# A head's cached keys loaded ahead of the ring into the memory of the attention's output, and a new order of score rows, maxima and query chunks

## The chip, the cores and the metric

The kernel runs on one core of a Trainium2 chip. Its engines are TensorE (PE in the profile; PEld is its weight load), VectorE (DVE), ScalarE (ACT), GpSimd (POOL) and SyncE (SP), which issues most of the loads from HBM. The metric is the device time of one execution in microseconds (us), less is better. The kernel before was run three times: 1280.98, 1282.48 and 1283.21 us, median 1282.48 us.

## The reference

One inference step of two layers for two groups of rows that share all weights: a prompt of 256 rows and 8 sample rows, each with its own cached keys and values. Each layer adds half a SwiGLU block, a mixer (a gated convolution in layer 0, a gated recurrence in layer 1), a cross attention over a memory, and another half SwiGLU block to the row:

```
for i in range(DEPTH):                                   # DEPTH = 2, D_MODEL = 1024, D_FF = 2816
    x = x + 0.5 * swiglu(rmsnorm(x, norm_ffn1[i]), ...)
    x = x + mixer_i(rmsnorm(x, norm_mix[i]))
    x = x + cross_attn(rmsnorm(x, norm_xattn[i]), mem_k[i], mem_v[i], w_xq[i], w_xo[i])
    x = x + 0.5 * swiglu(rmsnorm(x, norm_ffn2[i]), ...)

def cross_attn(x, mk, mv, w_q, w_o):                     # 4 heads of 256, 256 memory rows
    q = (x @ w_q).reshape(B, T, X_HEADS, X_HEAD_DIM)
    s = jnp.einsum('bthd,bnhd->bhtn', q, mk) / math.sqrt(X_HEAD_DIM)
    p = jax.nn.softmax(s, axis=-1)
    return jnp.einsum('bhtn,bnhd->bthd', p, mv).reshape(B, T, D) @ w_o
```

The prompt's memory keys and values are computed in the kernel (`rmsnorm(mem) @ w_kv`, 256 rows). The sample's keys and values are read from the caches, 8 batches x 256 rows x 4 heads x 256 numbers per layer, 8 MB of keys and 8 MB of values.

## The kernel before

All products run in three matmuls of rounded halves, hi x hi, lo x hi and hi x lo (`mm3`, L339 to L341; in the memory's keys and values L987 to L989). Each half chunk of weights is loaded by SP into `raw` (L99, six buffers), rounded by ACT into `wh` (L110), and the rest `wl` is made by DVE or POOL (L125; five buffers each). Prompt and sample rows stand side by side as 264 columns, so that PE has one stream of products from start to end; everything else is fitted between them.

The order is the program's order, as a scheduler with priorities lays it out, with some edges put in by hand (`order(...)`). Side work is written as generators in two lanes of a `Flow`; `flow.tick()` after every few products takes one step of each lane. So a `yield` is a unit of distance: what stands behind it comes one tick later in every engine's order.

The attention of a layer (about 300 to 425 us of the span in layer 0, 960 to 1085 in layer 1) runs so:

- `project` computes the queries, two chunks (two heads) at a time: k steps 0 to 2 of chunk 0, 0 to 2 of chunk 1, then the steps 3 to 7 of both in turn, then the evacuation of both by `evac_q` (L973), which starts the sample's score generator of the head in lane 0.
- `do_kv` computes keys and values of the prompt's memory, head by head, in two banks `kv`. Each head starts three generators in lane 1: `transpose_k` (`pkt` L1017, its copy `KTt` L1021), `prompt_scores` (matmuls `psc` L1070 into a bank, maxima `mxp` L1057 on DVE, two exponentials `Pp` on ACT, L315, reciprocal `zsp` L1060 on DVE, scaling `Pp` L1062 on ACT, transposes `ppt` L1084 on PE, its halves `PTh` and `PTl` L1091), and `prompt_values` (products `po`, outputs `oh` and `ol` L1107).
- `sample_scores(h)`, lane 0: a query transpose `pq` (L1038) and 16 rows on DVE (L1043, one row of keys of all 128 partitions against `pq`, a yield after every fifth), then the maximum `mxs` (L1050) and an exponential.
- `sample_rest`, lane 0, behind the four heads' scores: after SLACK = 5 yields, for each pair of heads 32 multiply-adds on DVE (L1153, L1156) into `acc` and, last, `total`; between them the steps of `combine`, which joins the maxima and sums of the partitions by small matmuls `pst` (L1112, L1119, L1129). Then the matmuls `spt<-oz,total` (L1173), which an edge holds behind the last product put out so far (`flow.passed`), and their evacuation `oh` (L1180, ACT) and `ol` (L1181, DVE).
- `out_proj` multiplies `oh`, `ol` with the output weights; its last two k steps wait for pair 1 of the sample.

The sample's keys and values come through a ring: four tiles of 1 MB, in the order k of heads 0 to 3 (two tiles each), then v of pairs 0 and 1 (four tiles each). `Ring.done` gives a tile back and at once issues the next load (`pump`), on SP, between the weight loads in program order. A load on SP waits until its tile is free and until one of eight outstanding loads has landed, and what stands behind it on SP waits too. The first tiles of a ring are issued while the stage before still runs.

Of the kernel before, what the change touches and what calls it, by code (L numbers as in the profile page):

```python
# [16 lines left out]
P = 128  # L17
# [22 lines left out]
HURRY = 40  # L40
STAGGER = 3
SLACK = 5
# [176 lines left out]
class Ring:  # L219


    def __init__(self, pool):
        self.pool, self.free, self.line, self.tiles, self.n = pool, RING, [], {}, 0

# [12 lines left out]

    def done(self, key):
        del self.tiles[key]
        self.free += 1  # L240
        self.pump()
# [3 lines left out]
def trunk_step(ctx: ExitStack, tc: tile.TileContext, ins, consts, outs, stop=None):  # L245
# [165 lines left out]
    def project(nch, rh, rl, evac, kt_major=2, need=None, before=None, late_lo=False):  # L411
        if not callable(rh):
            rh, rl = (lambda k, t=rh: t[:, k]), (lambda k, t=rl: t[:, k])
        done = 0
        if kt_major:
# [18 lines left out]
            else:  # L434
                order = [(c, k) for c in range(kt_major) for k in range(STAGGER)]
                order += [(c, k) for k in range(STAGGER, KT) for c in range(kt_major)]
                for n, (c, k) in enumerate(order):
                    if before is not None and c == 0:
                        before(k)
                    for j in range(2):  # L440
                        s = slice(j * P, j * P + P)
                        mm3(pss[2 * c + j][2][:, :NC], ws[c](k), rh(k), rl(k), k == 0, k == KT - 1, s)
# [6 lines left out]
            if need is not None:  # L449
                need.ready()  # L450
            with tc.high_priority(offset=HURRY):
                for c, j, ps in pss:
                    evac(c, j, ps[:, :NC])
# [312 lines left out]
    def add_cache(l):  # L766
# [15 lines left out]
        for h in range(XH):  # L782
            for hf in range(2):
                ring.add((l, "k", h, hf), fill_k(h, hf))
# [159 lines left out]
    def attention(l, norm, nxt):  # L944
        with tc.tile_pool(name="at", bufs=1) as ap:
# [83 lines left out]
            def sample_scores(h):  # L1029
# [10 lines left out]
                for i in range(NI):  # L1040
                    t = ring.tiles[l, "k", h, i // 8].rearrange("p (i d) -> p i d", d=XD)
                    junk = ap.tile([P, XD], F32, tag="junk", name="junk", bufs=1)
                    nc.vector.tensor_tensor_reduce(  # L1043
                        junk, t[:, i % 8], pq[:, :XD], 1.0, 0.0, ALU.mult, ALU.add, sc[:, h, i : i + 1]
                    )
# [7 lines left out]
            def softmax(src, npart, rows, name):  # L1053
# [3 lines left out]
                nc.vector.reduce_max(mx, src, axis=AX.X, negate=True)  # L1057
# [37 lines left out]
            def prompt_values(h):  # L1095
# [9 lines left out]
                ohv, olv = oh[:, 2 * h : 2 * h + 2, :T], ol[:, 2 * h : 2 * h + 2, :T]  # L1105
# [34 lines left out]
            def sample_rest():  # L1140
# [4 lines left out]
                for pair in range(XH // 2):  # L1145
# [31 lines left out]
                    with tc.high_priority(offset=HURRY):  # L1177
                        ptv = pt[:, : 4 * NB].rearrange("p (t b) -> p t b", b=NB)
                        ohv, olv = (t[:, 4 * pair : 4 * pair + 4, T:] for t in (oh, ol))
                        nc.scalar.copy(ohv, ptv)  # L1180
                        nc.vector.tensor_sub(olv, ptv, ohv.bitcast(F32))  # L1181
# [10 lines left out]
            project(XH, xh, xl, evac_q, need=norm)  # L1192
            for h in range(XH):
                do_kv(h)
            out_proj(oh, ol, nxt, late=(KT - 2, lambda k: until(k // 4), lambda: flow.drain(1)))
# [490 lines left out]
```

## Time and profile before

| | |
|---|---|
| three runs, us | 1280.98, 1282.48, 1283.21 |
| the profiled execution, us | 1282.15 |
| its span, us | 1280.4 |
| PE busy | 1258.7 us, 98% |
| DVE busy | 842.4 us, 66% |
| ACT busy | 703.4 us, 55% |
| POOL busy | 346.9 us, 27% |
| chain that ended last | PE 91%, DVE 3%, ACT 2%, DMA 2% |
| 1 MB loads of cached keys | 16, median 8.8 us from issue to landing |
| 1 MB loads of cached values | 16, median 9.1 us |

Busy times are of one profiled execution. The span runs from the first instruction to the last; the execution's own time is 1.75 us more. The clock column of a view by windows is the share of TensorE's clock that was granted in that window; over the whole span it was 0.997.

### The profile page before, as it was taken

The page shows a single profiled execution, that of the slowest core. Times are in us where ns is not written, and L with a number is a line of the kernel's source. Part 1 is how long each engine was busy: PE and PEld are TensorE (multiplying, and loading weights), DVE is VectorE, ACT ScalarE, POOL GpSimd, SP SyncE. Part 2 cuts the span into 40 slices and gives each one's busy share as a digit, 9 for nine tenths or more (in the row PEclk, how much of TensorE's full clock was granted, in tenths as well). Part 3 has the DMA queues.
Part 4 walks back from the last instruction along what each step waited for, and adds up shares of the span by engine and source line. Part 5 has one row for each costly group of instructions (what it writes and reads, how often), then busy time and mean ns, then how long its engine had stood idle before and what let it go on. Part 6 is the DMA issues. An engine that isn't in the chain of part 4 may idle for free.

```text
span 1280.4 us, 25535 instructions
## 1 busy us (share of the span) xinstructions
PE 1258.7 (98%) x10039; PEld 1230.7 (96%) x10039; DVE 842.4 (66%) x1625; ACT 703.4 (55%) x1167; POOL 346.9 (27%) x272
## 2 busy tenths in 40 slices
PE   8999999999999999999999999999999999999996
PEld 8999999999789999999999999999999789999996
DVE  7655567758777655546655535887887787766454
ACT  6455544446655645544555544656566666766542
POOL 2211231214864211132111132000016862112220
PEclk9999999999999999999999999999999999999999
DMA  8795556655899666556666556653545997997550
GB/s 274 246 305 177 167 180 190 187 160 178 295 395 318 193 176 189 172 168 191 193 173 191 171 171 190 193 171 122 189 151 172 385 384 248 287 324 227 162 165 35
DMA packets 269898, 270.96 MB, mean 212 GB/s; under 512 B 8777, under 2 KB 259721, under 8 KB 269266
## 3 DMA queue, kind: packets, MB, share of 16 engines
q1 hardware_dynamic: 263870, 263.98, 65.4%
q10 hardware_dynamic: 5908, 5.35, 1.2%
q8 instruction: 79, 1.29, 0.4%
q14 instruction: 41, 0.34, 0.1%
HBM read 259.19 MB, written 10.10 MB: 210 GB/s over the span
## 4 chain that ended last, share of the span: by engine, by line
PE 91%; DVE 3%; ACT 2%; DMA 2%; POOL 1%; issue 1%; SPq 0%; DVEq 0%; POOLq 0%; ACTq 0%
PE pj L340 20%; PE pj L339 20%; PE pj L341 20%; PE dn L339 7%; PE dn L341 7%; PE dn L340 7%; PE kv L987 2%; PE kv L988 2%; PE kv L989 2%; ACT wh L110 1%; DVE wl L125 1%; PE pl L1333 1%; PE psc L1070 1%; DMA ring<-in_cache_mem_k_dram 1%; DVE xl L365 1%; DMA raw<-in_w_xkv_dram 1%
## 5 line engine op out<-in xcount | busy, mean ns | idle before, releaser
L125 DVE TENSOR_TENSOR wl<-raw,wh 128x1024 fp32r<-128x1024 f32 (+1 forms) x334 | 411.7, 1238 | 240.0 <-ACT wh L110 224.2
L339 PE MATMUL pj<-xh,wh 128*128 128x264 f32 x1952 | 557.8, 286 | 0.3 <-DVE g L824 0.3
L340 PE MATMUL pj<-xl,wh 128*128 128x264 f32 x1952 | 553.4, 284 | 0.0
L341 PE MATMUL pj<-xh,wl 128*128 128x264 f32 x1952 | 553.0, 283 | 0.0
L110 ACT CAST wh<-raw 128x1024 fp32r<-128x1024 f32 (+1 forms) x406 | 415.5, 1032 | 215.9 <-PE pj L340 107.8
L339 PEld LDWEIGHTS pj<-xh,wh 128*128 128x128 f32 x1952 | 367.7, 188 | 1.9 <-issue 1.4
L340 PEld LDWEIGHTS pj<-xl,wh 128*128 128x128 f32 x1952 | 368.0, 189 | 0.2
L341 PEld LDWEIGHTS pj<-xh,wl 128*128 128x128 f32 x1952 | 366.1, 188 | 0.0
L125 POOL TENSOR_TENSOR wl<-raw,wh 128x1024 fp32r<-128x1024 f32 (+1 forms) x74 | 173.3, 2356 | 127.2 <-ACT wh L110 108.3
L832 POOL TENSOR_TENSOR al<-a,ah 128x264 fp32r<-128x264 f32 x88 | 90.4, 1029 | 411.2 <-ACT ah L831 411.1
L339 PE MATMUL dn<-ah,wh 128*128 128x264 f32 x704 | 200.9, 285 | 0.0
L341 PE MATMUL dn<-ah,wl 128*128 128x264 f32 x704 | 200.0, 284 | 0.0
L340 PE MATMUL dn<-al,wh 128*128 128x264 f32 x704 | 199.4, 283 | 0.0
L341 PEld LDWEIGHTS dn<-ah,wl 128*128 128x128 f32 x704 | 132.7, 188 | 0.0
L339 PEld LDWEIGHTS dn<-ah,wh 128*128 128x128 f32 x704 | 132.4, 188 | 0.2
L340 PEld LDWEIGHTS dn<-al,wh 128*128 128x128 f32 x704 | 132.5, 188 | 0.0
L315 ACT ACTIVATE g<-g 128x264 f32<-128x264 f32 x88 | 36.9, 424 | 76.6 <-DVE g L824 76.6
L831 ACT CAST ah<-a 128x264 fp32r<-128x264 f32 x88 | 36.0, 413 | 68.2 <-DVE a L830 68.1
L360 ACT ACTIVATE xh<-xT,gains 128x264 fp32r<-128x264 f32 x56 | 28.1, 512 | 72.0 <-DVE xT L858 59.1
L1043 DVE CUSTOM_DVE_ANT_0 junk<-ring,pq 128x256 f32<-128x256 f32 x128 | 53.7, 420 | 12.3 <-DMA ring<-in_cache_mem_k_dram 8.6
L378 POOL TENSOR_TENSOR nacc_norm_xattn<-nacc_norm_xattn,nsq 128x264 f32<-128x264 f32 x14 | 13.6, 972 | 174.8 <-ACT nsq L377 174.5
L1156 DVE SCALAR_TENSOR_TENSOR acc<-ring,sc,acc 128x256 f32<-128x256 f32 x112 | 54.5, 487 | 2.7
(327 smaller groups left out, 1538.7 us busy)
## 6 DMA issues: line engine op xcount, KB each, us to landing
raw<-in_w_ffn_gate_dram SPq DMA_DIRECT2D x88, 512.0 KB, 5.8
raw<-in_w_ffn_up_dram SPq DMA_DIRECT2D x88, 512.0 KB, 4.6
raw<-in_w_ffn_down_dram SPq DMA_DIRECT2D x64, 512.0 KB, 4.1
ring<-in_cache_mem_k_dram SPq DMA_DIRECT2D x16, 1024.0 KB, 8.8
raw<-in_w_xkv_dram SPq DMA_DIRECT2D x64, 256.0 KB, 3.6
ring<-in_cache_mem_v_dram SPq DMA_DIRECT2D x16, 1024.0 KB, 9.1
raw<-in_w_rec_in_dram SPq DMA_DIRECT2D x32, 512.0 KB, 4.3
raw<-in_w_ffn_down_dram SPq DMA_DIRECT2D x32, 384.0 KB, 3.0
```

What stands on the lines that cost most here:

```text
L110: ins = self.behind(self.hi[i % len(self.hi)], copy(wh[:, :n], self.raw[i][:, :n]))
L125: ins = eng.tensor_sub(wl[:, :n], self.raw.pop(i)[:, :n], wh[:, :n].bitcast(F32))
L315: in_line(nc.scalar.activation(dst, src, func, **kw))
L339: nc.tensor.matmul(ps, wh[:, s], rh, start=first, stop=False)
L340: nc.tensor.matmul(ps, wh[:, s], rl, start=False, stop=False)
L341: return nc.tensor.matmul(ps, wl[:, s], rh, start=False, stop=last).ins
L360: W.pin(nc.scalar.activation(xh[:, k, :n], src, AF.Copy, scale=gcol(self.name, self.layer, k)))
L831: nc.scalar.copy(ah[:, blk], a)
L832: nc.gpsimd.tensor_sub(al[:, blk], a, ah[:, blk].bitcast(F32))
L987: nc.tensor.matmul(pss[nt], mh[:, k, t], wh, start=k == 0, stop=False)
L1043: nc.vector.tensor_tensor_reduce(junk, t[:, i % 8], pq[:, :XD], 1.0, 0.0, ALU.mult, ALU.add, sc[:, h, i : i + 1])
L1156: nc.vector.scalar_tensor_tensor(dst, t[:, i % 4, j], p, sums, op0=ALU.mult, op1=ALU.add)
```

## The change

Four things are changed in the attention, the same in both layers. No arithmetic is added or taken away, and the same bytes are loaded.

First, the two key tiles of head 2 (`GUEST`) no longer pass through the ring. When the attention starts, two tiles `spare0` and `spare1` are opened under the same tags as the outputs `oh` and `ol`, with one buffer each, and head 2's keys are loaded into them (`Ring.lodge`). The outputs are opened in the same memory when the first prompt head writes them. The ring then carries the keys of heads 0, 1 and 3, and after them the values, so that each load behind head 1 moves two places forward.

Second, a row of sample scores on DVE comes behind the last `mxp` of the program so far (`ahead`), and the generator yields after every fourth row rather than every fifth. SLACK is 1 in place of 5.

Third, in the query projection, chunk 0 computes its k steps 5 to 7 in one piece and is evacuated before chunk 1 does its own (`split=5`); before, both ended together.

Fourth, the `wl` splits that DVE does later come behind the sample's `ol` (`W.after["v"]`).

```
-SLACK = 5
+GUEST = 2
+SLACK = 1
 class Ring:
+        self.guests, self.lodged = {}, set()
+    def lodge(self, key, t):
+        self.guests.pop(key)(t)
+        self.tiles[key] = t
+        self.lodged.add(key)
     def done(self, key):
         del self.tiles[key]
+        if key in self.lodged:
+            return
         self.free += 1
         self.pump()
...
-    def project(nch, rh, rl, evac, kt_major=2, need=None, before=None, late_lo=False):
+    def project(nch, rh, rl, evac, kt_major=2, need=None, before=None, late_lo=False, split=KT):
+        def out(c):
+            if need is not None:
+                need.ready()
+            with tc.high_priority(offset=HURRY):
+                for j in range(2):
+                    evac(c, j, pss[2 * c + j][2][:, :NC])
...
-                order += [(c, k) for k in range(STAGGER, KT) for c in range(kt_major)]
+                order += [(c, k) for k in range(STAGGER, split) for c in range(kt_major)]
+                order += [(c, k) for c in range(kt_major) for k in range(split, KT)]
...
+                    if split < KT and k == KT - 1:
+                        out(c)
...
-                ring.add((l, "k", h, hf), fill_k(h, hf))
+                if h == GUEST:
+                    ring.guests[l, "k", h, hf] = fill_k(h, hf)
+                else:
+                    ring.add((l, "k", h, hf), fill_k(h, hf))
...
-            oh = ap.tile([P, KT, NC], F32R, name="oh")
-            ol = ap.tile([P, KT, NC], F32R, name="ol")
+            both = {}
+            for hf, tag in enumerate("hl"):
+                t = ap.tile([P, KT, NC], F32, tag="o" + tag, name=f"spare{hf}", bufs=1)
+                ring.lodge((l, "k", GUEST, hf), t.rearrange("p k n -> p (k n)")[:, : 8 * XD])
+            def open_out():
+                for tag in "hl":
+                    both[tag] = ap.tile([P, KT, NC], F32R, tag="o" + tag, name="o" + tag, bufs=1)
...
-            sampled = set()
+            sampled, ahead = set(), []
...
+                    if ahead:
+                        order(row, ahead[-1], "heads ahead of rows")
...
-                    if i % 5 == 4:
+                    if i % 4 == 3:
                         yield
...
-                nc.vector.reduce_max(mx, src, axis=AX.X, negate=True)
+                ahead.append(nc.vector.reduce_max(mx, src, axis=AX.X, negate=True).ins)
...
+                if not both:
+                    open_out()
...
-                        nc.vector.tensor_sub(olv, ptv, ohv.bitcast(F32))
+                        W.after["v"] = nc.vector.tensor_sub(olv, ptv, ohv.bitcast(F32)).ins
...
-            project(XH, xh, xl, evac_q, need=norm)
+            project(XH, xh, xl, evac_q, need=norm, split=5)
```

The kernel's lines move by some 30: the score row is L1043 before and L1075 now, `mxp` L1057 and L1091, `zsp` L1060 and L1094, `psc` L1070 and L1104, `ppt` L1084 and L1118, `spt` L1173 and L1209.

**SP's queue in layer 0's attention, before.** `raw` are halves of weights, `ring9` to `ring12` the key tiles of heads 2 and 3, `ring13` and `ring14` the first two value tiles:

```order
L770 DMA ring9_4084<-in_cache_mem_k_dram 128x8x256
L99 DMA raw116_4144<-in_w_xkv_dram 128x2x256 x2
L770 DMA ring10_4149<-in_cache_mem_k_dram 128x8x256
L99 DMA raw117_4212<-in_w_xkv_dram 128x2x256 x2
L770 DMA ring11_4221<-in_cache_mem_k_dram 128x8x256
L99 DMA raw118_4235<-in_w_xkv_dram 128x2x256 x2
L770 DMA ring12_4258<-in_cache_mem_k_dram 128x8x256
L99 DMA raw119_4272<-in_w_xkv_dram 128x2x256 x2
L99 DMA raw120_4304<-in_w_xkv_dram 128x2x256 x2
L778 DMA ring13_4313<-in_cache_mem_v_dram 128x4x512
L99 DMA raw121_4359<-in_w_xkv_dram 128x2x256 x2
L778 DMA ring14_4364<-in_cache_mem_v_dram 128x4x512
```

The same queue now, at the attention's start and then around head 3's keys and the first values; the row behind the last one shown is `raw120`:

```order
L100 DMA raw108_3776<-in_w_xkv_dram 128x2x256 x2
L792 DMA spare0_3821<-in_cache_mem_k_dram 128x8x256
L792 DMA spare1_3823<-in_cache_mem_k_dram 128x8x256
L100 DMA raw109_3852<-in_w_xkv_dram 128x2x256 x2
L100 DMA raw110_3869<-in_w_xkv_dram 128x2x256 x2
```

```order
L792 DMA ring9_4067<-in_cache_mem_k_dram 128x8x256
L100 DMA raw115_4117<-in_w_xkv_dram 128x2x256 x2
L792 DMA ring10_4128<-in_cache_mem_k_dram 128x8x256
L100 DMA raw116_4150<-in_w_xkv_dram 128x2x256 x2
L100 DMA raw117_4212<-in_w_xkv_dram 128x2x256 x2
L800 DMA ring11_4223<-in_cache_mem_v_dram 128x4x512
L100 DMA raw118_4233<-in_w_xkv_dram 128x2x256 x2
L800 DMA ring12_4260<-in_cache_mem_v_dram 128x4x512
L100 DMA raw119_4270<-in_w_xkv_dram 128x2x256 x2
```

Head 2's two loads stand six weight halves further up, directly behind the first half of the key-value weights; head 3's two take the places in the ring that head 2's had, and the first two value loads those of head 3's. The third value load, before between the key-value weights `raw122` and `raw123`, stands behind the first half of the output weights, `raw124`, now, and the fourth behind the second.

**DVE's queue at head 3's first rows, layer 0.** `sc` are the scores (each row is two instructions there), `mxs` is head 2's maximum, `mxp` the maxima of the prompt's first head. Before:

```order
L1050 TENSOR_REDUCE mxs<-sc 128x1
L1043 ISA junk,sc<-ring_4221,pq 128x256
L1043 ISA sc 128x1
L1043 ISA junk,sc<-ring_4221,pq 128x256
L1043 ISA sc 128x1
L1043 ISA junk,sc<-ring_4221,pq 128x256
L1043 ISA sc 128x1
L1043 ISA junk,sc<-ring_4221,pq 128x256
L1043 ISA sc 128x1
L1057 TENSOR_REDUCE mxp<-psc 128x2
```

Now:

```order
L1084 TENSOR_REDUCE mxs<-sc 128x1
L1091 TENSOR_REDUCE mxp<-psc 128x2
L1075 ISA junk,sc<-ring_4067,pq 128x256
L1075 ISA sc 128x1
L1075 ISA junk,sc<-ring_4067,pq 128x256
L1075 ISA sc 128x1
L1075 ISA junk,sc<-ring_4067,pq 128x256
L1075 ISA sc 128x1
L1094 RECIPROCAL zsp<-zsp 128x2
```

Four rows of head 3 went from ahead of `mxp` to behind it, and the reciprocal stands three rows behind `mxp` as before.

**PE's queue where pair 0 of the sample is handed over, layer 0.** `psc` are head 2's prompt scores, `kv3` head 3's key and value products. Before:

```order
L1070 MATMUL psc_4762<-KTt2_4746,qT2_4022 128x256 x4
L987 MATMUL kv3_0_4723<-wh121_4581,mh_3819 128x512
L988 MATMUL kv3_0_4723<-wl121_4611,mh_3819 128x512
L989 MATMUL kv3_0_4723<-wh121_4581,ml_3820 128x512
L987 MATMUL kv3_1_4724<-wh121_4581,mh_3819 128x512
L988 MATMUL kv3_1_4724<-wl121_4611,mh_3819 128x512
L989 MATMUL kv3_1_4724<-wh121_4581,ml_3820 128x512
L1173 MATMUL spt_4786<-oz_3824,total_4570 128x8 x4
```

Now:

```order
L1021 MATMUL kv3_1_4730<-wh121_4589,ml_3820 128x512
L1209 MATMUL spt_4762<-oz_3826,total_4557 128x8 x2
L1104 MATMUL psc_4769<-KTt2_4746,qT2_4027 128x256
L1209 MATMUL spt_4762<-oz_3826,total_4557 128x8 x2
L1104 MATMUL psc_4769<-KTt2_4746,qT2_4027 128x256 x3
L1019 MATMUL kv3_0_4729<-wh121_4589,mh_3819 128x512
```

The sample's matmuls went from six products behind head 2's scores to the place at which these scores stood, ahead of and among them. Layer 1 has the same rows in the same order at all of these places.

More of the change, by code (lines that the diff above doesn't have):

```diff
@@ L441, in project @@
                         s = slice(j * P, j * P + P)
-                        mm3(pss[2 * c + j][2][:, :NC], ws[c](k), rh(k), rl(k), k == 0, k == KT - 1, s)
+                        flow.passed = mm3(
+                            pss[2 * c + j][2][:, :NC], ws[c](k), rh(k), rl(k), k == 0, k == KT - 1, s
+                        )
+                    if split < KT and k == KT - 1:
+                        out(c)
                     if n % kt_major == kt_major - 1:
@@ L448, in project @@
             W.release()
[L449 to L453, printed above, removed]
+            if split == KT:
+                for c in range(kt_major):
+                    out(c)
             flow.tick()
@@ L1042, in sample_scores @@
                     junk = ap.tile([P, XD], F32, tag="junk", name="junk", bufs=1)
-                    nc.vector.tensor_tensor_reduce(
+                    row = nc.vector.tensor_tensor_reduce(
                         junk, t[:, i % 8], pq[:, :XD], 1.0, 0.0, ALU.mult, ALU.add, sc[:, h, i : i + 1]
                     )
+                    if ahead:
+                        order(row, ahead[-1], "heads ahead of rows")
                     if i % 8 == 7:
                         ring.done((l, "k", h, i // 8))
-                    if i % 5 == 4:
+                    if i % 4 == 3:
                         yield
@@ L1104, in prompt_values @@
                 pov = po.rearrange("p (t n) -> p t n", t=2)
-                ohv, olv = oh[:, 2 * h : 2 * h + 2, :T], ol[:, 2 * h : 2 * h + 2, :T]
+                if not both:
+                    open_out()
+                ohv, olv = (both[tag][:, 2 * h : 2 * h + 2, :T] for tag in "hl")
                 nc.scalar.copy(ohv, pov)
@@ L1178, in sample_rest @@
                         ptv = pt[:, : 4 * NB].rearrange("p (t b) -> p t b", b=NB)
-                        ohv, olv = (t[:, 4 * pair : 4 * pair + 4, T:] for t in (oh, ol))
+                        ohv, olv = (both[tag][:, 4 * pair : 4 * pair + 4, T:] for tag in "hl")
                         nc.scalar.copy(ohv, ptv)
-                        nc.vector.tensor_sub(olv, ptv, ohv.bitcast(F32))
+                        W.after["v"] = nc.vector.tensor_sub(olv, ptv, ohv.bitcast(F32)).ins
                     sampled.add(pair)
@@ L1191, in attention @@
             flow.spawn(1, mem_split())
-            project(XH, xh, xl, evac_q, need=norm)
+            project(XH, xh, xl, evac_q, need=norm, split=5)
             for h in range(XH):
                 do_kv(h)
-            out_proj(oh, ol, nxt, late=(KT - 2, lambda k: until(k // 4), lambda: flow.drain(1)))
+            out_proj(both["h"], both["l"], nxt, late=(KT - 2, lambda k: until(k // 4), lambda: flow.drain(1)))
     GH = 4
```

## The prediction

> **What bounds the kernel now.** I read the page's busy times and its chain of waits first, then PE's waits, and then single instructions around the two longest.
>
> ```profile
> PE 1258.7 (98%) x10039; PEld 1230.7 (96%) x10039; DVE 842.4 (66%) x1625; ACT 703.4 (55%) x1167; POOL 346.9 (27%) x272
> PE 91%; DVE 3%; ACT 2%; DMA 2%; POOL 1%; issue 1%; SPq 0%; DVEq 0%; POOLq 0%; ACTq 0%
> PE ppt L1084 <- ACT Pp L1062: 3.6, 2, 2.3
> PE pj L340 <- DVE ol L1181: 1.4, 2, 0.7
> PE pj L339 <- ACT oh L1180: 0.5, 2, 0.3
> PE psc L1070 <- ACT KTt L1021: 0.3, 1, 0.3
> ```
>
> PE is busy for 98%, and no product is added or removed, so only PE's idle time and its slow time can move the end. The last four rows (PE's waits: total us, times, longest) are what the attentions hold: 3.6 us in which the transposes `ppt` of the first prompt head wait for its scaled probabilities, once in each layer, and 1.9 us at the end of each attention's products for the sample's outputs (1.4 for `ol`, 0.5 for `oh`). The chain that leads to the longer one, layer 0:
>
> ```profile
> 341.52 1.99 PE L1070 MATMUL psc<-KTt,qT 128*128 128x256 f32 x8 [0.35 <-ACT KTt L1021]
> 345.11 0.42 DVE L1043 CUSTOM_DVE_ANT_0 junk<-ring,pq 128x256 f32<-128x256 f32 x1 [2.19 <-DMA ring<-in_cache_mem_k_dram]
> 346.85 0.69 DVE L1057 TENSOR_REDUCE mxp<-psc 128x2 f32<-128x512 f32 x1
> 347.26 0.39 PE L989 MATMUL kv<-wh,ml 128*128 128x512 f32 x1
> 347.57 0.47 ACT L315 ACTIVATE Pp<-psc,mxp 128x256 f32<-128x256 f32 x1 [4.21 <-DVE mxp L1057]
> 348.48 1.04 ACT L110 CAST wh<-raw 128x1024 fp32r<-128x1024 f32 x1
> 349.41 0.91 ACT L1062 ACTIVATE Pp<-Pp,zsp 128x256 f32<-128x256 f32 x2
> 349.98 1.30 PE L1084 MATMUL ppt<-ident,Pp 128*128 128x128 f32 x4 [2.33 <-ACT Pp L1062]
> ```
>
> The scores are there at 341.52 + 1.99 = 343.51, and their maximum starts at 346.85. In between DVE stood at head 3's first row, which waited 2.19 us for its keys, and did four such rows, since they are ahead of `mxp` in its order. From `mxp` everything follows at once, 3.13 us to `ppt`; PE was out of work at 347.26 + 0.39 = 347.65. Layer 1 is the same with shorter waits, 1000.34 + 1.95 = 1002.29 against 1004.56:
>
> ```profile
> 1000.34 1.95 PE L1070 MATMUL psc<-KTt,qT 128*128 128x256 f32 x8
> 1002.82 0.42 DVE L1043 CUSTOM_DVE_ANT_0 junk<-ring,pq 128x256 f32<-128x256 f32 x1 [1.13 <-DMA ring<-in_cache_mem_k_dram]
> 1004.56 0.69 DVE L1057 TENSOR_REDUCE mxp<-psc 128x2 f32<-128x512 f32 x1
> 1007.70 0.94 PE L1084 MATMUL ppt<-ident,Pp 128*128 128x128 f32 x4 [1.30 <-ACT Pp L1062]
> ```
>
> **What the stall costs.** In windows (us, then busy time of PE, PEld, DVE, ACT, POOL with counts, granted clock, DMA share, GB/s):
>
> ```profile
> 347.60:350.00 2.40, 0.07 (x2) 0.02 (x1) 2.26 (x12) 2.40 (x7) 0.40 (x1) 0.98 1.09 388
> 350.00:353.40 3.40, 3.40 (x10) 2.71 (x11) 3.22 (x14) 1.85 (x3) 3.40 (x2) 0.51 1.06 398
> 1007.70:1011.00 3.30, 3.23 (x15) 2.59 (x16) 3.07 (x14) 2.11 (x4) 3.13 (x2) 1.00 1.07 403
> ```
>
> Behind layer 0's gap the clock is granted at 0.51 for 3.40 us, which costs 3.40 x (1 - 0.51) = 1.67 us more; behind the gap of 1.30 us in layer 1 it stays at 1.00. So layer 0's stall is worth 2.33 + 1.67 = 4.00 us and layer 1's 1.30.
>
> That the low clock goes with the gap is read from these two windows alone. The Trainium skill ("TensorE: Matmul & The Clock Gate", Part 1, "What's actually happening") has the clock fall after at least one idle window of about 3.4 us, which runs freely; a gap of 2.33 us would not fill one. By that page the low stretch has another cause and could stay, and the sum would lose its 1.67 us; the trace speaks against it as far as one row can, since the low clock begins where the gap ends.
>
> **Maxima ahead of rows.** The new edge puts `mxp` ahead of head 3's rows. By 345.11 - 2.19 = 342.92 DVE had ended head 2 in layer 0, by 1002.82 - 1.13 = 1001.69 in layer 1, both ahead of the scores' ends, so `mxp` can start at 343.51 and 1002.29, 3.34 and 2.27 us sooner, whatever the loads do. The three rows between `mxp` and `zsp` stay. With the same 3.13 and 3.14 us behind it `ppt` is ready at 346.64 and 1005.43. PE comes to it at 347.65, and in layer 1 at 1007.70 - 1.30 = 1006.40. Both stalls are gone with 1.0 us to spare; a row of 0.42 us or half the weight cast (1.04 us, ahead of `Pp` on ACT) would still fit. Gain: 4.00 + 1.30 = **5.3 us**.
>
> **Head 2's keys ahead of the ring; four rows a step; split queries.** These bring nothing by themselves: they move the sample's chain on DVE forward, and its cover is that DVE then idles at `mxp`. They matter for what follows. The loads:
>
> ```profile
> 306.00:312.00 6.00, 6.00 (x50) 5.86 (x49) 4.46 (x7) 4.21 (x8) 0.62 (x1) 1.00 0.55 172
> 312.00:327.00 15.00, 15.00 (x119) 14.64 (x118) 11.54 (x50) 10.81 (x23) 12.82 (x11) 1.00 0.43 140
> 334.16 0.57 SPq L770 DMA_DIRECT2D ring<-in_cache_mem_k_dram  x1
> 346.25 0.37 SPq L778 DMA_DIRECT2D ring<-in_cache_mem_v_dram  x1
> 351.77 0.40 SPq L778 DMA_DIRECT2D ring<-in_cache_mem_v_dram  x1
> 359.02 1.07 SPq L99 DMA_DIRECT2D raw<-in_w_xo_dram  x1
> L125 POOL TENSOR_TENSOR wl<-raw,wh 128x1024 fp32r<-128x1024 f32 (+1 forms) x74 | 173.3, 2356 | 127.2 <-ACT wh L110 108.3
> ```
>
> The two spare loads (2 MB) go where the DMA share is 0.55 and 0.43, so the weights behind them on SP are not made late; in exchange head 3's second load (334.16) and the first value load (346.25) start when the slots two places ahead come free, by head 1's rows rather than head 2's, 16 rows of 0.42 us or 6.7 us sooner at least. The spare tiles wait for the last readers of the outputs' memory, the stage before, so SP isn't held. Where this leaves a loss is the third value load (351.77): it now stands behind the first output weight half on SP, which was issued at 359.02. It needs the buffer that POOL's split behind the cast of 348.48 frees, and before it also stood behind a fourth value load that waited for its ring slot. With `mxp` 3.34 us sooner the cast is at 345.14 to 346.18, and with one or two splits of 2.36 us (last row, the page's group) the buffer is free by 348.5 to 350.9; the fourth value load is now behind it. I put the third value load at about 351, where it is now.
>
> **The sample's handover, one step of order sooner.** SLACK 1 puts `spt` where `psc` of head 2 begins:
>
> ```profile
> 376.59 1.89 PE L1070 MATMUL psc<-KTt,qT 128*128 128x256 f32 x8
> 379.70 0.95 PE L1173 MATMUL spt<-oz,total 128*128 128x8 f32 x8
> 376.84 0.87 DVE L1156 SCALAR_TENSOR_TENSOR total<-ring,sc,acc 128x256 f32<-128x256 f32 x2
> 1032.93 1.89 PE L1070 MATMUL psc<-KTt,qT 128*128 128x256 f32 x8
> 1033.17 0.87 DVE L1156 SCALAR_TENSOR_TENSOR total<-ring,sc,acc 128x256 f32<-128x256 f32 x2
> DVE ol L1107 <- ACT oh L1106: 2.3, 1, 2.3
> DVE pst L1115 <- PE pst L1112: 0.8, 1, 0.8
> DVE acc L1153 <- DMA ring<-in_cache_mem_v_dram: 0.7, 1, 0.7
> DVE mxp L1057 <- PE psc L1070: 0.5, 1, 0.5
> DVE PTl L1091 <- ACT PTh L1090: 0.4, 1, 0.4
> ```
>
> Here is the new wait. PE comes to it at 376.59 - 4.00 = 372.6 and 1032.93 - 1.30 = 1031.6. Behind it PE queues head 2's scores and all later products, and their `mxp` and `ppt`. DVE had `total` ready at 376.84 + 0.87 = 377.71 and 1034.04. From head 3's first row to there it took 32.6 us in layer 0, with the last five rows' 4.7 us of waits in it, so 27.9 us of work. Now the same work begins with `mxp` at 343.51 (1002.29): 371.4 and 1030.2 without any wait; 376.1 if all of them stay, and in layer 1, where it took 31.2 us in all, 1033.5. The largest, for `ol` and `pst`, are waits for PE, which itself comes 4.0 us sooner in layer 0 while the rows do not, and `ol` stands behind three more rows; the one for values falls with the earlier load. So I expect 0 to 0.5 us of waiting per layer and take **0.2 each**; the far end is 376.1 - 372.6 = 3.5 and 1.9 us. The matmuls of `combine`, sooner in order too, I bound from 0 to the 0.8 us that DVE waited at `pst`, and take **0.1 for both layers**, as DVE runs beside PE here.
>
> **The end of the attention.** `spt` of pair 1 now stands ahead of the last `ppt`, so more products lie between it and the two waits of 0.5 and 1.4 us; and the sample's `ol` stands ahead of this split on DVE:
>
> ```profile
> 400.12 2.19 DVE L125 TENSOR_TENSOR wl<-raw,wh 128x1024 fp32r<-128x1024 f32 x1 [0.76 <-ACT wh L110]
> ```
>
> Before, `ol` had to sit out its 2.19 us. With the split behind it, `ol` needs its own short subtraction only. From nothing to all of 1.9 us; I take **1.6 us** for the two layers, the rest for a split of `wl` that comes later, which the products behind cover as long as it is under a weight half of lead.
>
> **The sum.** 5.3 + 1.6 - 0.4 - 0.1 = 6.4 us. The profiled execution took 1282.15 us (span 1280.4, 1.75 around it); 1282.15 - 6.4 = 1275.75, and as the median of the runs is 0.33 above that execution, the median is **1276.1 us**. Bounds: 5.3 + 1.9 = 7.2 us at most by these rows, to which some tenths may come where matmuls merely start late, and 5.3 - 0.6 if the end brings nothing; so 1274.8 to 1277.8 us for this case.
>
> **Rivals.**
>
> *The sample's chain becomes the bound.* DVE keeps all its waits, and PE stands at `spt` for 3.5 and 1.9 us: 5.4 of the 6.8 us gained elsewhere are given back, 1281.1 us. With three quarters of the waits kept it is 371.4 + 3.5 - 372.6 = 2.3 us and 1030.2 + 2.5 - 1031.6 = 1.1 us, 1279.1 us. I put 1280. For it: the handover moved up by one step of order, and PE by 4 us besides, so that the lead on paper is 1.2 and 1.4 us only. Against: the waits are for PE and for loads, which both move forward.
>
> *Something else holds `Pp`.* If the cast of 1.04 us ahead of `Pp` on ACT waits for a weight buffer that only PE's later products free, `ppt` comes as late as now. Then only the end's 1.6 us is gained, less the 0.4 and 0.1: 1281.4 us. For it: the cast stands there; against: at 348.48 it began the moment the exponentials ended.
>
> *The low clock isn't the gap's.* The stretch at 0.51 stays somewhere: 6.4 - 1.67 = 4.7 us, 1277.8 us. By the rows alone a small chance. The Trainium skill's window of 3.4 us, above, is the case for it.
>
> *Slower: the third value load.* If SP's queue stays as late as now, the output weight half is issued at 359.02 and the value tile behind it, to land at about 368 (the page's median for a 1 MB value load is 9.1 us). DVE needs it half way through pair 0's 32 rows, by the sum above about 363. Then `total` is 5 us late, PE idles for 371.4 + 5 - 372.6 = 3.8 us in layer 0 and 1030.2 + 5 - 1031.6 = 3.6 us in layer 1, and after gaps of that size 1.67 us of low clock each: 10.7 us against the 6.8, 1286.4 us. It costs from 1.2 us of lateness on, and turns the result from about 3 us. Against it: what held that half, a cast and a value load ahead of it, has moved.
>
> **How the numbers follow.** Forecast 0.58 (1276.1); chain as bound 0.13, of which half within 0.2%; `Pp` held 0.11 (same); clock 0.07 (faster); slower 0.09; 0.02 is left over, half of it faster, half slower. A measurement of this kernel tells 0.2% (2.6 us) from no change. Faster: 0.58 + 0.06 + 0.07 + 0.01 = 0.72; within: 0.07 + 0.11 = 0.18; slower: 0.09 + 0.01 = 0.10. The range leaves out the slower case and, at the lower edge, a gain beyond the rows' bound of 7.2 us with some tenths for late starts: 1273.6 to 1281.6 us.
>
> **What would show it.** In the profile after: no wait of `ppt` for `Pp` over 0.3 us in either layer, `mxp` within 0.1 us of the end of `psc`, the clock at 1.00 from 347 to 354; a waiting time of at most 0.5 us at `spt`; loads of head 2's keys in the stretch around 303 to 327; 0.4 us or less in all at `oh` and `ol`. A wait of `spt` for `total` over 1.5 us, or of DVE for values, would make the prediction wrong, and so would the same ends with PE's idle time merely moved into the products behind.

## The result, and the profile after

The changed kernel takes 1272.80 us (median of six runs, 1272.71 to 1273.11), the kernel before beside it 1281.31 us (six runs, 1280.15 to 1283.21): a ratio of 0.9933, 95% interval 0.992 to 0.9946, 8.5 us less. The forecast was 1276.1 us and the range 1273.6 to 1281.6. The sign and the largest term were right, the time lies 0.8 us below the range. The profiled execution took 1272.73 us, its span is 1270.9 us against 1280.4.

The page's busy times and chain of the kernel after, then PE's waits over the whole execution (total us, times, longest):

```profile
PE 1254.6 (99%) x10039; PEld 1229.2 (97%) x10039; DVE 841.0 (66%) x1625; ACT 703.4 (55%) x1167; POOL 346.1 (27%) x272
PE 96%; DVE 2%; ACT 1%; issue 1%; DMA 0%; POOL 0%; DVEq 0%; SPq 0%; POOLq 0%
```

```profile
PE pr L610 <- DMA ring<-in_x_sample_dram: 2.8, 1, 2.8
PE px L633 <- DMA ring<-in_x_prompt_dram: 1.0, 1, 1.0
PE pfa L1620 <- DVE xT L883: 1.0, 1, 1.0
PE pj L350 <- DVE ol L1217: 0.9, 1, 0.9
```

The waits of `ppt` (3.6 us before), of `psc` and for `oh` are gone; of the end's waits one of 0.9 us for `ol` is left, in layer 1. The other rows lie at the program's start and end. PE's busy time fell by 4.1 us though it does the same 10039 matmuls: part of it is the stretch at half clock in layer 0's attention, which is gone too. The place where the stall was, in the timeline

```profile
340.85 1.89 PE L1104 MATMUL psc<-KTt,qT 128*128 128x256 f32 x8
342.78 0.69 DVE L1091 TENSOR_REDUCE mxp<-psc 128x2 f32<-128x512 f32 x1 [3.07 <-PE psc L1104]
346.71 0.60 PE L1118 MATMUL ppt<-ident,Pp 128*128 128x128 f32 x4
```

and in windows:

```profile
340.00:347.00 7.00, 7.00 (x35) 5.82 (x34) 4.01 (x18) 3.85 (x10) 7.00 (x5) 1.00 1.07 388
347.00:353.40 6.40, 6.40 (x38) 5.53 (x37) 5.51 (x24) 4.67 (x8) 5.56 (x4) 1.00 1.05 349
```

DVE is now the one that waits, 3.07 us, and `mxp` starts 0.04 us behind the end of `psc`; `ppt` follows the products without a gap, PE is busy in every microsecond of the two windows, and the clock is 1.00. Note also that `psc` itself starts without a wait; it had waited 0.35 us for `KTt`. The handover in both layers:

```profile
371.52 0.51 PE L1209 MATMUL spt<-oz,total 128*128 128x8 f32 x4
370.29 0.86 DVE L1192 SCALAR_TENSOR_TENSOR total<-ring,sc,acc 128x256 f32<-128x256 f32 x2
1024.19 0.51 PE L1209 MATMUL spt<-oz,total 128*128 128x8 f32 x4
1022.96 0.86 DVE L1192 SCALAR_TENSOR_TENSOR total<-ring,sc,acc 128x256 f32<-128x256 f32 x2
```

`total` is ready at 371.15 and 1023.82, PE comes 0.37 us later each time: no wait, and little to spare.

Counted by the start of the same matmul in both traces (how many us earlier it starts in the kernel after), the 9.5 us of the spans' difference came so: 0.25 us in the program's start; in layer 0's attention 0.58 at `psc`, 4.19 from `ppt` to the end of the low clock, 0.1 around `spt`, 1.45 at the end; in layer 1's 0.3 ahead of it, 1.80 at `ppt`, 0.1 in between and 0.41 at the end; 0.3 us in the program's tail.

### The profile page after: what moved, and what is told of

It reads as the page before. It is cut to its first block, busy times and chain, and to the rows that moved or that the text cites. A ratio compares the mean times of both kernels' runs of the same rounds, so it can differ in the third digit from the quotient of the medians.

```text
span 1270.9 us, 25527 instructions
## 1 busy us (share of the span) xinstructions
PE 1254.6 (99%) x10039; PEld 1229.2 (97%) x10039; DVE 841.0 (66%) x1625; ACT 703.4 (55%) x1167; POOL 346.1 (27%) x272
## 4 chain that ended last, share of the span: by engine, by line
PE 96%; DVE 2%; ACT 1%; issue 1%; DMA 0%; POOL 0%; DVEq 0%; SPq 0%; POOLq 0%
PE pj L349 21%; PE pj L350 21%; PE pj L351 20%; PE dn L349 7%; PE dn L351 7%; PE dn L350 7%; PE kv L1019 2%; PE kv L1021 2%; PE kv L1020 2%; PE psc L1104 1%; PE pl L1369 1%; DVE wl L126 0%; ACT wh L111 0%; DVE xl L375 0%; PE pl L1352 0%
## 5 line engine op out<-in xcount | busy, mean ns | idle before, releaser
L370 ACT ACTIVATE xh<-xT,gains 128x264 fp32r<-128x264 f32 x56 | 27.9, 513 | 72.5 <-DVE xT L883 59.2
L849 DVE TENSOR_TENSOR g<-pj,R_norm_ffn 128x264 f32<-128x264 f32 x88 | 37.5, 429 | 28.7 <-PE pj L351 28.5
```

What stands on the lines that cost most here:

```text
L370: W.pin(nc.scalar.activation(xh[:, k, :n], src, AF.Copy, scale=gcol(self.name, self.layer, k)))
L849: nc.vector.tensor_mul(g, ps, norm.R)
```

## The experiments

The medians below are compared with runs of the kernel before on the same chip, which moved between 1280.6 and 1282.6 us from chip to chip; so ratios, not times, are compared across them.

### The orders alone

`order_only`: the kernel before with `SLACK = 1`, a yield after every fourth row, and the edge that holds rows behind the last `mxp`.

```
-SLACK = 5
+SLACK = 1
-                    if i % 5 == 4:
+                    if i % 4 == 3:
...
+                    if ahead:
+                        order(row, ahead[-1], "heads ahead of rows")
```

> The kernel before with the orders alone: rows behind the last mxp, a step of four rows, SLACK 1. The loads, the queries and the output's splits stay as before. Theory (the place of mxp in DVE's order sets the stall): DVE is done with head 2 before the scores are, so mxp starts within 0.1 us of the end of psc, the waits of ppt (2.3 and 1.3 us) and the stretch of low clock go; head 3's keys still land at about 345, so total comes at 373 to 377 us against PE at about 375.5 at spt, a new wait of 0 to 1.5 us in layer 0, none in layer 1; the end's waits of 1.9 us stay. Gain 4.5 to 6 us, 1275.3 to 1276.8 us. Rival (the late keys are what holds the kernel, the order only shifts the wait): gain under 1.5 us, with a wait at spt of more than 3 us.

Measured: 1282.47 us, ratio 0.9996 (0.9987 to 1.0005). Nothing is gained. The rival had the size, but not the place: PE doesn't wait at `spt`. The rows that tell why: from PE's waits, then from ACT's timeline.

```profile
PE psc L1072 <- ACT KTt L1021: 3.7, 2, 1.9
```

```profile
340.52 0.62 ACT L1004 CAST Vh<-Vn 128x512 fp32r<-128x512 f32 x1 [3.37 <-DMA raw<-in_w_xkv_dram]
341.99 0.58 ACT L1021 COPY KTt<-pkt 128x512 f32<-128x512 f32 x1
```

The waits of `ppt`, 3.6 us in two, are gone as the theory had it; in their place `psc`, one step ahead, waits 3.7 us in two. `KTt` is late because ACT stood 3.37 us between `Vn` and `Vh`. What lies there are two instructions that are not counted as busy, the issues of the stores of the prompt's memory keys and values (L1001). In each trace the DMAs that SP and ACT issue signal on the same eight semaphores, in turn, and ahead of each of these two issues ACT waits for the semaphore that the store will use, until the DMA that had it before has landed. Here the store of the keys goes out at 338.78, behind a cached-key load that landed at 338.70, and that of the values at 340.07, behind a weight load that landed at 340.00 (by the trace's semaphore events). Before, ACT stood there too, 2.1 us in layer 0, and of that 0.35 us reached PE:

```profile
ACT Vh L1004 <- DMA ring<-in_cache_mem_k_dram: 2.1, 1, 2.1
```

### The keys alone

`only_guest`: head 2's keys ahead of the ring, all else as before.

```
 SLACK = 5
+                if h == GUEST:
+                    ring.guests[l, "k", h, hf] = fill_k(h, hf)
...
+                ring.lodge((l, "k", GUEST, hf), t.rearrange("p k n -> p (k n)")[:, : 8 * XD])
```

> The kernel before with head 2's keys loaded ahead of the ring alone: five rows a step, SLACK 5, no order of rows behind maxima, both query chunks ending together, no order of the splits behind ol. Theory: the keys of head 3 are there when head 2 ends, so the four rows ahead of mxp are done before psc ends, and mxp starts at the end of psc although nothing was put ahead of it; the waits of ppt and the low clock go, the end's waits of 1.9 us stay: gain 5.5 to 6.5 us, 1274.8 to 1275.8 us. Rival (the order of rows and maxima is needed): mxp stays over 1 us behind psc, gain under 2 us.

Measured: 1280.8 us, ratio 0.9985 (0.9976 to 0.9993): a gain of 1.9 us by the ratio, 1.5 by the medians. The wait at `ppt` is gone here as well, with four rows of head 3 still ahead of `mxp`: the theory's first half holds. The second half, its size, does not. The rest of the stall is spread over other waits:

```profile
PE pj L350 <- DVE ol L1215: 1.6, 2, 0.9
PE psc L1102 <- ACT KTt L1053: 0.8, 1, 0.8
PE po L350 <- DVE PTl L1123: 0.7, 2, 0.3
PE pj L349 <- ACT oh L1214: 0.6, 2, 0.3
```

### The changed kernel without one of its parts

`no_edge`: without the edge of rows behind `mxp`.

```
-                    if ahead:
-                        order(row, ahead[-1], "heads ahead of rows")
```

> The changed kernel without the edge that holds rows behind the last mxp; four rows of head 3 then stand ahead of mxp again. Theory (keys and edge each suffice): those rows are done before psc ends, mxp and ppt as in the changed kernel, time 1272.3 to 1273.5 us. Rival (the edge carries the gain): ppt waits again for 1 us or more in each layer, 1276 us or more.

Measured: 1272.66 us, ratio 0.9926 (0.9914 to 0.9938), the changed kernel's time. Four rows stand ahead of `mxp` again, and cost nothing, since they are done within 0.1 us of the scores' end. The edge carries none of the gain once the keys are early.

`no_guest`: with head 2's keys in the ring.

```
-                if h == GUEST:
-                    ring.guests[l, "k", h, hf] = fill_k(h, hf)
-                else:
-                    ring.add((l, "k", h, hf), fill_k(h, hf))
+                ring.add((l, "k", h, hf), fill_k(h, hf))
```

> The changed kernel with head 2's keys back in the ring, all orders as changed. Theory: mxp at the end of psc and no wait at ppt, but head 3's rows wait for keys until about 345, total comes 1 to 2 us later than in the changed kernel while spt stands ahead of head 2's scores: PE waits there 0.5 to 3 us in layer 0 and 0 to 1 us in layer 1; 1273.5 to 1277 us. Rival (the loads carry the whole gain): 1278 us or more, the waits at ppt back. Rival (the loads bring nothing): 1272.5 to 1273.2 us.

Measured: 1274.65 us, ratio 0.994 (0.9928 to 0.9952): about 2 us of the gain goes. The time is within the theory's range, the place is not: PE doesn't wait at `spt`, but at the small matmuls that join the sample's maxima and sums, 1.0 us idle in all. Counted by the start of the same matmul, these places cost 1.1 us in layer 0 and 1.7 in layer 1 against the changed kernel, and the end of layer 1 gives 0.9 back.

```profile
PE pst L1142 <- DVE mxs L1078: 0.8, 2, 0.4
...
PE pst L1159 <- DVE zss L1156: 0.2, 1, 0.2
```

`no_split`: both query chunks end together.

```
-            project(XH, xh, xl, evac_q, need=norm, split=5)
+            project(XH, xh, xl, evac_q, need=norm)
```

> The changed kernel with both query chunks ending together as before. Theory: head 0's rows start 1.4 us later, which DVE's idle time ahead of mxp (3.07 us) covers; but the sample's chain loses one step of order, spt stands behind psc and, at the end, behind ppt again, so 0.4 to 1.2 us of the end's waits come back: 1273.2 to 1274.2 us. Rival (split gives nothing at all): 1272.5 to 1273.0 us. Rival (the split query is what takes the KTt wait of layer 0 away): psc waits 0.3 to 0.6 us again.

Measured: 1278.78 us (1277.59 to 1282.15), ratio 0.9982 (0.9972 to 0.9992). That misses all three in size: some 6 us of the changed kernel's 8.5 hang on the order of 36 matmuls a layer. The third had the place. The profile has the same wait as the orders alone, and the same stand on ACT (the last row is of layer 0 alone, the others of both layers):

```profile
PE psc L1104 <- ACT KTt L1053: 3.6, 2, 1.9
PE pj L349 <- ACT oh L1216: 0.6, 2, 0.3
...
ACT Vh L1036 <- DMA raw<-in_w_xkv_dram: 3.4, 1, 3.4
```

In the changed kernel's trace this stand is 0.7 us, the two issues themselves.

`no_after`: without the order of `wl` splits behind `ol`.

```
-                        W.after["v"] = nc.vector.tensor_sub(olv, ptv, ohv.bitcast(F32)).ins
+                        nc.vector.tensor_sub(olv, ptv, ohv.bitcast(F32))
```

> The changed kernel without the order of wl splits behind the sample's ol. Theory: in layer 0 one split (about 2 us there) is ahead of ol on DVE again, and the products wait for ol for 0.5 to 0.9 us; layer 1 has no split ahead of ol either way: 1273.3 to 1273.8 us. Rival (PE's 24 products cover the split): 1272.5 to 1273.0 us, no wait for ol in layer 0.

Measured: 1274.55 us, ratio 0.9951 (0.9938 to 0.9963). That is some 1.7 us more than the changed kernel, beyond both ranges. PE waits 1.3 us for `ol` in layer 0, more than expected, and a stretch of low clock follows it in the profiled execution:

```profile
396.30:397.60 1.30, 0.04 (x2) 0.02 (x1) 1.30 (x3) 0.00 (x0) 0.04 (x1) 0.92 1.17 291
397.60:401.00 3.40, 3.40 (x16) 3.40 (x17) 0.52 (x1) 0.00 (x0) 0.00 (x0) 0.53 1.20 290
```

`slack5`: SLACK 5 again.

```
-SLACK = 1
+SLACK = 5
```

> The changed kernel with SLACK 5. Each head's rows now take four steps, not three, so with SLACK 5 the hand-over comes four steps later than with 1: spt of pair 0 stands 25 products further down and that of pair 1 behind 12 products more. Theory: no wait at pair 0's spt in either, but the end is later: the last products wait 1 to 2 us for oh and ol in each layer: 1275 to 1276.5 us. Rival (the handover's place does not matter): 1272.5 to 1273.2 us.

Measured: 1290.88 us (1288.66 to 1294.35), ratio 1.0075 (1.0061 to 1.0088): slower than the kernel before by 10 us. The direction was expected, the size not. The waits:

```profile
PE po L349 <- DVE PTl L1125: 7.2, 2, 5.5
PE spt L1209 <- DVE total L1192: 4.3, 2, 2.4
```

With four steps a head instead of three the sample's chain takes four steps more to lay out, so SLACK 1 is not an earlier handover: it keeps the old place, and SLACK 5 puts it four steps later, where the last products must wait for the sample, and DVE does its rows ahead of `PTl`. The six products by which `spt` stands sooner in the changed kernel come with the split queries: in `no_split` it stands six products behind `psc`, as before. Four rows a step was not undone by itself.

### What the split queries do

Two kernels take the stand away from ACT by itself. `order_store` is `order_only` with both stores moved behind the copy `KTt`, in the generator `transpose_k`:

```
-                for dram, t in ((new_k, kn), (new_v, vn)):
-                    nc.scalar.dma_start(dram[l, 0, :, h].rearrange("(t p) d -> p t d", p=P), t)
                 vh = ap.tile([P, 2, XD], F32R, tag="Vh", name=f"Vh{h}", bufs=1)
...
                 nc.scalar.copy(KTt[h], pt.rearrange("p (t n) -> p t n", t=2))
+                for dram, t in ((new_k, kn), (new_v, vn)):
+                    nc.scalar.dma_start(dram[l, 0, :, h].rearrange("(t p) d -> p t d", p=P), t)
```

> The kernel with the orders alone (order_only), and the stores of the prompt's memory keys and values issued by ACT behind the copy KTt instead of ahead of Vh. In order_only ACT stood 3.4 us in each layer at these two stores, between Vn and Vh, and psc waited about 2 us for KTt. Theory (the stores' issue holds ACT until an earlier load has landed, and that is where the orders' gain went): Vh and KTt come 2 to 3 us sooner, psc's waits go to under 0.3 us, ppt's stay gone, the end's waits of 1.3 us a layer stay: 3 to 6 us less than before, 1276 to 1279 us. Rival (KTt is late because its transposes or Vh are, whatever the stores do): psc waits as long, 1281 to 1283 us.

Measured: 1278.76 us, ratio 0.9978 (0.9969 to 0.9987): 3.6 us less than before by the medians, 2.8 by the ratio. The waits of `psc` are gone, as the theory had it; with late keys DVE comes late to `PTl`, and the end's waits are as before:

```profile
PE po L340 <- DVE PTl L1093: 2.1, 3, 1.1
PE pj L340 <- DVE ol L1183: 1.4, 2, 0.7
...
PE pj L339 <- ACT oh L1182: 0.6, 2, 0.3
```

`no_split_store` is `no_split` with the same move of the stores.

> The changed kernel with both query chunks ending together (no_split) and the two stores of the prompt's memory keys and values behind the copy KTt on ACT. no_split lost 6 us against the changed kernel, with psc waiting 1.9 us in each layer while ACT stood 3.4 us at these stores. Theory (the split queries bring their gain by what ACT's stores meet, nothing else): psc's waits go, the end's wait for oh of 0.3 us a layer stays: 1273.0 to 1275.0 us. Rival (the split's gain lies in head 0's earlier start or in the handover's place): 1276.5 us or more, with a wait at spt, pst or PTl of 1.5 us or more.

Measured: 1273.39 us (1273.11 to 1273.91), ratio 0.9928 (0.9914 to 0.9942). Without the split, and with the handover where it was before, 0.5 to 0.6 us are left of the 6. What PE waits for here and not in the changed kernel is `oh` at the end, and `PTl` once:

```profile
PE pj L349 <- ACT oh L1216: 0.5, 2, 0.3
...
PE po L350 <- DVE PTl L1125: 0.3, 1, 0.3
```

So the split brings its gain by what ACT's stores meet. That is shown, but for one pairing that was not run, the split together with the moved stores; in the changed kernel `psc` waits for nothing, so the move has nothing to take away there.

How it does so can be read from the turns of the eight semaphores. In `no_split`, layer 0, the load of head 3's second key tile and the two stores:

```profile
329.49 1.94 SPq L792 DMA_DIRECT2D ring<-in_cache_mem_k_dram  x1
338.99 0.42 ACTq L1033 DMA_DIRECT2D out_dram<-Kn  x1
340.26 0.40 ACTq L1033 DMA_DIRECT2D out_dram<-Vn  x1
```

The first store uses the semaphore of that key load, 1 MB, which landed at 338.92; the second that of a weight load which landed at 340.18. Each goes out 0.07 to 0.08 us later. In the changed kernel the second value load stands ahead of the stores and takes that key load's semaphore. The stores take the next ones, of two weight loads that landed at 334.43 and 335.06, and the first goes out without a wait:

```profile
336.81 0.42 ACTq L1033 DMA_DIRECT2D out_dram<-Kn  x1
```

Layer 1 shows the same in both kernels (a key load that landed at 994.21 ahead of a store at 994.29; two weight loads that had landed over a microsecond before).

### The low clock, and the kernel before again

`before_again` is the kernel before, unchanged, and profiled once more.

> The kernel before, unchanged, profiled again. Theory (the low clock is drawn by where a gap falls on a free-running window, so its place changes from run to run while the gaps do not): the gaps of 2.3, 1.3 and about 1.3 us stand where they did within 0.3 us, stretches of low clock of 3.4 us stand behind another of them, or behind none, or two, and the time moves by 1.7 us for each. Rival (the long gap of layer 0 always brings it): exactly one such stretch, behind ppt of layer 0, again.

Measured: 1281.03 us. No stretch of low clock stands in its attentions at all. The rival is out, and half of the theory's first sentence: the gap at layer 0's `ppt` is not a constant of the kernel, it was 1.4 us here and 2.3 in the first profile, while `psc` waited 1.1 us in two instead of 0.3:

```profile
PE ppt L1084 <- ACT Pp L1062: 2.6, 2, 1.4
PE pj L340 <- DVE ol L1181: 1.4, 2, 0.7
PE psc L1070 <- ACT KTt L1021: 1.1, 2, 0.6
```

```profile
347.60:349.00 1.40, 0.20 (x1) 0.00 (x0) 0.92 (x6) 1.40 (x4) 0.20 (x1) 1.00 1.09 380
349.00:353.40 4.40, 4.15 (x22) 3.43 (x23) 4.11 (x18) 3.21 (x7) 4.28 (x2) 1.00 1.07 399
```

That alike gaps can come with the low clock or without it is seen best within one execution, in `order_only`, whose two waits of `psc` are alike:

```profile
340.80:342.60 1.80, 0.02 (x1) 0.00 (x0) 1.66 (x9) 1.80 (x4) 1.50 (x3) 1.00 1.09 366
342.60:346.00 3.40, 3.38 (x17) 2.87 (x17) 0.80 (x2) 1.83 (x6) 3.40 (x2) 1.00 1.09 380
...
998.90:1000.80 1.90, 0.05 (x2) 0.01 (x1) 1.75 (x10) 1.90 (x4) 1.49 (x3) 1.00 1.09 367
1001.00:1004.40 3.40, 3.40 (x9) 2.69 (x9) 0.00 (x0) 0.99 (x3) 3.40 (x2) 0.51 1.09 384
```

Idle for 1.8 us, then full clock; idle for 1.9 us, then 3.4 us at half. The same execution has one more such stretch, from 400.29, behind no more than the waits for `oh` and `ol` at the end of layer 0's attention, 0.3 and 0.7 us.

The theory's other half, windows that run freely, is borne out by the clock's records: 400.29 and 1001.04 lie 600.75 us apart, 176.0 times 3.413 us, and wherever an execution has several low stretches they start whole multiples of that apart. On this grid the gap of 1.85 us ahead of 1001.04 lies in one window; the other, 1.80 us, is cut in two, 1.45 and 0.35 us. So where a gap falls matters. How much idle time a window takes is open: 1.85 and 2.27 us brought the low clock, 1.45 us did not, but at the end of the attention 0.97 us did here and 0.98 us did not in `before_again`.

### A version that is faster still

The wait of 0.9 us for `ol` that is left in layer 1 has its cause on DVE:

```profile
1047.00 1.95 DVE L1562 SCALAR_TENSOR_TENSOR ring<-ring,ks,ring 128x128 f32<-128x128 f32 x1 [1.87 <-ACT ring L325]
1048.87 0.18 DVE L1217 TENSOR_TENSOR ol<-spt,oh 128x32 fp32r<-128x32 f32 x1
1044.09 4.72 POOL L126 TENSOR_TENSOR wl<-raw,wh 128x1024 fp32r<-128x1024 f32 x2 [3.86 <-DMA raw<-in_w_ffn_up_dram]
```

An update of the sample's recurrence state, which belongs to later work, stands ahead of `ol`. `state_late` puts all these updates behind it:

```
-                    nc.vector.scalar_tensor_tensor(
+                    upd = nc.vector.scalar_tensor_tensor(
                         S0[:, hh, b], v[:, hh, b], ks[:, h, b : b + 1], S0[:, hh, b], op0=ALU.mult, op1=ALU.add
                     )
+                    order(upd, flow.handed, "sample's output ahead of states")
...
+                    flow.handed = W.after["v"]
                     sampled.add(pair)
```

> The changed kernel with one more order: the updates of the sample's recurrence states on DVE come behind the sample's ol of the attention. In the changed kernel's trace the first of them starts at 1047.00 and takes 1.95 us (the median of 64 is 0.347 us) while POOL runs a split, and ol behind it ends at 1049.05, for which PE waits 0.87 us. Theory: that update is what holds ol; without it ol follows oh at about 1047.7 and PE's wait goes: 1271.8 to 1272.1 us. Rival (ol is held by POOL's split itself or by oh): ol as late, 1272.6 to 1273.0 us.

Measured: 1271.92 us, ratio 0.9929 (0.9916 to 0.9941). Then beside the changed kernel on one chip:

> The changed kernel, unchanged, beside the next one on the same chip: 1272.6 to 1273.2 us, no gap over 1.1 us in the attentions and no stretch of low clock there.

> The changed kernel with the recurrence states' updates behind the sample's ol, timed beside the changed kernel on the same chip. Theory: 0.7 to 1.1 us less than the changed kernel in every pair of medians. Rival: within 0.3 us of it.

Measured: 1272.93 us for the changed kernel (1272.72 to 1274.05; ratio 0.9929, 0.9915 to 0.9942) and 1271.96 us for this one (1271.75 to 1273.11; ratio 0.9921, 0.9909 to 0.9934): 0.97 us less by the medians, as expected. PE's wait for `ol` is gone from its list of waits, and `ol` starts 0.22 us behind `oh`:

```profile
1047.85 0.19 ACT L1216 CAST oh<-spt 128x32 fp32r<-128x32 f32 x1 [0.52 <-PE spt L1209]
1048.07 0.19 DVE L1217 TENSOR_TENSOR ol<-spt,oh 128x32 fp32r<-128x32 f32 x1 [2.58 <-ACT oh L1216]
1048.17 1.15 DVE L1563 SCALAR_TENSOR_TENSOR ring<-ring,ks,ring 128x128 f32<-128x128 f32 x1
```

## Why the prediction was right or wrong

**What bounds the kernel, and what the stall costs: right.** The gain came from PE's idle and slow time in the attentions, and the gap and its low clock in layer 0 came to 4.19 us against 4.00 forecast. That so close a fit came out is partly luck: 1.67 of it is a low stretch that this one execution happened to have. Counted from `before_again`, which has none in its attentions, to the changed kernel, the same place gives 1.88 us in layer 0 and 1.71 in layer 1, and `psc` 0.74 and 0.80. Layer 1's gap was undersized, 1.80 against 1.30: the forecast took the idle time of the row (1.30) and left out that the transposes behind a gap start slowly, which the start-to-start count has in it.

**"Maxima ahead of rows": the size was right, the cause named for it wrong.** The step said that the new edge frees `mxp` "whatever the loads do". `no_edge` has the whole gain without the edge, and `order_only` has the freed `mxp` and no gain. What failed in it is the sentence that takes the end of `psc` as given: with `mxp` out of the way the chain is held one step further up, at `KTt`.

**"These bring nothing by themselves": wrong, and the step that failed most.** For the split queries and the early keys the forecast looked only at DVE's idle time. `no_split` showed that the split carries some 6 us: without it ACT stands 3.4 us at the two stores in each layer, and `psc` waits 3.6 us in all for `KTt`. The keys carry some 2 us (`no_guest`). These are losses when one part is taken out of the whole, and don't add up. The 0.58 us that `psc` gained in layer 0 is the visible part of this, and had no term in the sum; its wait stood in the rows quoted there, 0.35 us, and was not followed back to ACT.

**The loads: right.** The third value load was put at about 351; it was issued at 349.86. The slower rival did not come.

```profile
349.86 0.46 SPq L800 DMA_DIRECT2D ring<-in_cache_mem_v_dram  x1
```

**The handover: right in mechanism, its cost too high.** From `mxp` to `total` without any wait of DVE was put at 27.9 us. It took 28.4 us in both layers (342.78 to 371.15 and 995.45 to 1023.82), 0.5 us above the bound, and the 0.4 us of waiting and the 0.1 at the small matmuls were not paid. But SLACK was read as a step sooner; by `slack5` it is what keeps the handover in place now that the rows take a step more a head, and the step sooner is the split's.

**The end: 1.6 forecast, 1.86 measured** (1.45 + 0.41), and not evenly: in layer 1 the wait for `ol` stayed, behind a state update that was not in that place before.

**The sum.** By terms: 4.19 + 1.80 + 1.86 + 0.58 = 8.4 us against 6.4. The 2.0 us between them are 0.7 at the stalls, 0.3 at the end, 0.6 at `psc` and the 0.5 that was charged and not paid. The further 1.0 us between the two profiled executions is 0.2 around `spt` and some 0.8 outside the attentions, whose cause is open; and 0.3 us is the median's distance to the first profile, which was added to the forecast and did not hold (the kernel before had 1281.31 in six runs, 1282.48 in three). So 2.0 + 1.0 + 0.3 makes the 3.3 us by which 1272.8 lies below 1276.1. The lower end of the range held to the waits that the one profile showed; it left out that a chain with stops at several places gives more when all of them go, and that gaps cost a varying amount.

**The clock.** The Trainium skill ("TensorE: Matmul & The Clock Gate", Part 1, "What's actually happening") wants at least one idle window of about 3.4 us, and has the windows run freely. The runs show stretches of that length, 3.41 us, and their starts on one grid; but they stand behind gaps of 1.3, 1.9 and 2.3 us and, in `order_only`, behind 0.3 and 0.7 us together, and alike gaps stand without any. The length and the grid agree with the page, the condition does not.

## What to carry to other kernels

When a wait is removed, follow each input of the instruction that waited one step further back and ask what will be late next, also what stands in an engine's queue without being busy: a DMA issue on ACT can hold the copies behind it for microseconds. Parts of a change that look idle by one engine's slack may act through another queue, so undo each of them alone before one is credited. Gaps on TensorE of one to two microseconds can cost 1.7 us more than their length, and they make the time scatter: 23 runs of the kernel before spread over 3.9 us, eleven of the changed kernel over 1.3 us.

## What the runs showed of the hardware that was not expected

**DMA issues on ACT.** The two stores behind `Vn` held ACT for 0.7, 1.5 to 2.5 and 3.3 to 3.4 us in kernels that differ only in the order of their work and loads, because each waits until the DMA that used its semaphore before, one of eight shared with SP, has landed. Where a store was held it went out 0.07 to 0.08 us behind that landing.

**Half clock by where a gap falls.** The low clock lasts 3.41 us in these attentions, 3.40 x (1 - 0.51) = 1.67 us lost, behind gaps of 1.3 to 2.3 us that elsewhere have none, and in `order_only`, `order_store` and `only_guest` behind 0.97 to 0.99 us at the end of layer 0's attention. In `slack5`, with gaps of up to 5.5 us, it lasts 6.83 and 13.65 us. The kernel before scatters accordingly: in 23 runs on one chip from 1280.51 to 1284.38 us, where the seven with a mean clock of 0.994 took 1283.8 us on the mean and the six with 0.997 took 1281.4.

**DVE beside POOL.** The state update took 1.95 us where the median of 64 is 0.347, and ended at 1048.95, with POOL's second split (1044.09 + 4.72 = 1048.81). Moved to 1048.17 it took 1.15 us and ended again with POOL's split of that run (1044.45 + 4.73 = 1049.18). The Trainium skill ("SBUF — State Buffer", "Who interferes with whom") says that a DVE instruction with two SBUF inputs contends with a GpSimd instruction that reads SBUF, and that the port pair which they share is an exclusive lock. Both rows agree with that, since the update ends 0.14 us behind POOL's split each time; that it is this lock, and not something else that POOL's split holds up, was not tried by itself. The update's durations in the changed kernel (minimum, median, maximum in ns), and POOL's splits in the version with the update moved:

```profile
L1562 DVE SCALAR_TENSOR_TENSOR ring<-ring,ks,ring x64: 335/347/1953, 1047.0 to 1157.5; 128x128 f32<-128x128 f32 x64
```

```profile
1044.45 4.73 POOL L126 TENSOR_TENSOR wl<-raw,wh 128x1024 fp32r<-128x1024 f32 x2 [3.86 <-DMA raw<-in_w_ffn_up_dram]
```
